# Moving two operands ahead of the last chunk's splits in the first quarter of an MLP, and two collections behind an operand in the last

## The chip, the cores and the metric

The kernel runs on one core of a Trainium2 chip. The metric is the device time of one execution in microseconds (us). The engines that matter are TensorE (PE, with its weight loads as PEld), VectorE (DVE), ScalarE (ACT), GpSimd (POOL) and SyncE (SP), each with its own queue of instructions that it takes in order; an instruction whose inputs or whose output buffer aren't ready holds up everything behind it on its engine.

## The reference

A two-layer encoder in float32 with S = 512 positions and a width of D = 1024. Layer 0 mixes with a stick-breaking attention, layer 1 with a gated linear recurrence (RG-LRU). The change touches the MLP that follows each of them:

```python
def squared_relu_mlp(h, w1, w2):
    u = jax.nn.relu(h @ w1)          # 512x1024 @ 1024x4096
    return (u * u) @ w2              # 512x4096 @ 4096x1024
...
        h = rms_norm(x, norm_mlp[layer])
        x = x + squared_relu_mlp(h, mlp_w1[layer], mlp_w2[layer])
    return rms_norm(x, norm_final)
```

## The kernel before

**Operands.** Every product is made from operands that are split in two halves: the high one is a cast on ACT (`wh`, `sh`, `bh`, `s`), the low one is what is left, a subtraction on DVE (`wl`, `sl`, `bl`, `low`). A product of a block takes three matmuls, high by high, low by high, high by low. So each operand costs one instruction on ACT and then one on DVE before PE can use it.

**Slots.** The halves of all weights live in tiles of the tags `wh` and `wl`. These come from one pool that has four slots for each tag (L91), and a new tile takes the slot of the tile four requests earlier, in the order in which the program requests them. The cast that fills a slot waits until PE has read the older tile for the last time.

**Quarters.** An MLP goes through the 4096 inner columns in four quarters (`q4` 0 to 3), the first of them in another form than the rest. In the first quarter `quarters` calls `squared` for eight chunks of 128 columns of `u`: 24 matmuls (`dense`, L236 to L238) with weights that `slab` loads, casts (L229, ACT) and subtracts (L231, DVE), then relu and square on ACT. After a pair of chunks `split` makes the halves of `u`, and `sums` forms differences of its parts for seven products (P1 to P7) that take the place of eight. `run` does what follows: the last chunk's `squared(C - 1)` with its splits and sums, the "down" products of the first quarter, and then "up" and "down" of the other three.

**Steps of `run`.** A down step multiplies one operand with the split `u` (12 matmuls of 128x512, recorded at L1107). `make(i)` builds the operand of step `i`: `operand` requests `wh` and `wl`, casts and subtracts. `add` forms a sum of two weight blocks `b` on DVE first, where the product needs one. `leave(i)` runs behind step `i`: it collects finished sums (`collect`: on DVE a multiply and add into `c` out of PSUM, or on ACT a scaled copy) and prepares the operand of step `i + 4`. Steps of the first quarter go P1 0, P5 0, P1 1, P2 0, P5 1 and so on (the number is the group of rows); steps of layer 1's last quarter go P1 0, P5 0, P1 1, P2 0, P5 1, P2 1, P6 0, P6 1, P3 0, P3 1, P7 0, P7 1, P4 0, P4 1.

**Order.** A scheduler places the instructions of each engine. Between `e.turn(True)` and `e.turn(False)` the MLP's own instructions on DVE and ACT are tied in the order in which the code issues them (`Ordered`); what is issued before that, and what doesn't go through `self.V` and `self.A` (the slab's L229 and L231 among it), may be placed between them. All operations that go through `Ordered` are recorded at L776, so they are told apart by their tiles.

In this text chunk 6 and chunk 7 are the last two chunks of `u` in the first quarter, and operands 0 to 4 are those of the first down steps.

Of the kernel before, what the change touches and what calls it, by code (L numbers as in the profile page):

```python
# [62 lines left out]
def hybrid_encoder(  # L63
# [72 lines left out]
    def x_down(*down):  # L136

        xgh.down = xgl.down = down
# [78 lines left out]
    behind = [None]  # L217
# [545 lines left out]
    NQ = DFF // D  # L763
# [22 lines left out]
    class Mlp:  # L786
# [357 lines left out]
        def run(self, first, between, end):  # L1144
# [13 lines left out]
            def place(i):  # L1158

                return (i + self.STEPS // 2) % self.STEPS  # L1160

            def unit(i):
                kind, q4, g, _ = steps[i]
                return units[kind, q4][g]
# [4 lines left out]
            def add(i, ahead=1):  # L1169

                if i >= len(steps) or i in done or steps[i][3] not in ("P5", "P6"):
                    return
                *what, name = steps[i]
                far = what[0] == "down" and (name, what[2]) in FARS
                if ahead > (5 if far else 2 if name == "P5" else what[0] == "up"):
                    return
                if steps.index((*what, {"P5": "P1", "P6": "P5"}[name])) in made:
                    done.add(i)

                    self.added(unit(i), name, far=far)  # L1180

            def make(i):
                if i >= len(steps):
                    return
                name = steps[i][3]
                ws[i] = made[i] = self.operand(self.source(unit(i), name))

                for before, x in (("P5", "P7"), ("P6", "P4")):
                    if name == before:
                        self.added(unit(i), x)  # L1190

            def prepare(i):

                if i < len(steps) and steps[i][0] == "up" and steps[i][3] == "P7":
                    return
                if i - 1 in range(len(steps)) and i - 1 not in made and i > 2:
                    make(i - 1)
                if i < len(steps) and steps[i][0] == "down":
                    add(i, 0)
                    if waiting and place(i) in (20, 22, 23):  # L1200
                        self.split_slot(*waiting.pop(0))
                make(i)
                for n in range(i + 1, i + 6):
                    add(n, n - i)

            def last_sums(u, which):
                for to, a, b, how in which:
                    self.V.tensor_tensor(u[to], u[a], u[b], how)
# [23 lines left out]
            def leave(i):  # L1232

                ahead = i + 4
                if i < 0:
                    return
                kind, q4, p, name = steps[i]
                bank = sums[kind, q4, p if kind == "up" else 0][self.PRODUCTS[name][3]]
                if kind == "down":
                    if q4 == 0 and self.s3 and place(i) in self.REPLACE:  # L1240
                        self.replace()
                    if p:
                        self.collect(name, 0, bank[0])
                    if steps[min(ahead, len(steps) - 1)][0] == "down":
                        add(ahead, 0)
                    if p:
                        self.collect(name, 1, bank[1])
                    prepare(ahead)
                    if later and place(i) > 15:
                        later.pop()()  # L1250
                    if q4 == 0:
                        x_down(FRONT, ASIDE)
                        if place(i) in self.LOWER:
                            self.lower(*self.LOWER[place(i)])

                        if self.layer == 0 and place(i) in (19, 20):
                            (self.sums_of_x, self.halves_of_sums)[place(i) - 19](3)
                    return
                u, three = us[p], bank.rearrange("p (i n) -> p i n", i=2)
                keep = {"P1": 0, "P6": 1, "P5": 2, "P7": 3}.get(name)  # L1260
                if keep is not None:

                    self.A.copy(u[keep], three)
                at, x, y, op = {
                    "P3": (1, three, u[1], ALU.subtract),
                    "P7": (2, u[2], u[3], ALU.subtract),
                    "P2": (0, u[0], three, ALU.add),
                    "P4": (3, three, None, None),
                }.get(name, (None,) * 4)
                if op:  # L1270
                    self.V.tensor_tensor(u[at], x, y, op)
                if name == "P4":
                    def fourth(u=u, three=three, p=p):
                        self.A.activation(u[3], three, AF.Relu)
                        self.square(u[3])
                        if p:
                            last_sums(u, self.SUMS[:2])
                        else:
                            self.sums(p, slice(0, 2))

                    if p:
                        fourth()
                    else:
                        later.append(fourth)
                elif later:
                    later.pop()()
                prepare(ahead)
                if op:
                    def rest(u=u, at=at):
                        self.A.activation(u[at], u[at], AF.Relu)  # L1290
                        self.square(u[at])
                        if p:
                            self.split_slot(p, u[at], at)

                    if p and name == "P3":
                        later.append(rest)
                    else:
                        rest()
                    if name == "P2" and not p:
                        self.split(p, slice(0, 2), slice(0, 3), slice(0, 3))  # L1300
                elif name == "P4" and p:
                    last_sums(u, self.SUMS[2:3])
                    self.split_slot(p, u[2], 5)
                    later.append(lambda: last_sums(u, self.SUMS[3:]))
                    waiting[:] = [(p, u[j], 3 + j) for j in (0, 1, 3)]
                elif name in ("P5", "P6") and p:
                    n = ("P5", "P6").index(name)
                    self.split(0, n, slice(0, 4), slice(3, 7))
# [3 lines left out]
            add(1)  # L1312
            make(1)
            add(5, 4)
            for e in (self.V, self.A):
                e.turn(True)
            self.squared(C - 1)
            self.split(1, 1, slice(0, 3), slice(0, 3))
            make(2)
            self.sums(1, 1)  # L1320
            make(3)
            add(4, 2)
            self.split(1, 1, slice(0, 4), slice(3, 7))
            between(C - 1)
            for i, (kind, q4, g, name) in enumerate(steps):
                load(i)
                leave(i - 1)
                if i == len(steps) - 2:
                    break
                if kind == "down":  # L1330
                    self.part(sums.setdefault((kind, q4, 0), {}), name, g, ws.pop(i))
                    continue
                if name == "P1":
                    us[g] = self.slots_of(g)
                banks = sums.setdefault((kind, q4, g), {})
                to = self.PRODUCTS[name][3]
                new = to not in banks
                if new:
                    banks[to] = self.bank()
                self.up(name, ws.pop(i), banks[to], new)  # L1340
# [490 lines left out]
```

## Time and profile before

| | before |
|---|---|
| time, median of 3 runs | 1032.02 us (1031.94 to 1032.03) |
| the profiled execution's own time | 1031.83 us |
| its span in the trace | 1030.1 us |
| mean granted TensorE clock | 0.999 |
| PE busy | 1021.6 us (99%) |
| PEld busy | 892.9 us (87%) |
| DVE busy | 859.7 us (83%) |
| ACT busy | 714.7 us (69%) |
| POOL busy | 173.9 us (17%) |

Rows of the timeline give the start in us from the span's start, the duration in us, engine, line, operation, the tile written and the tiles read, shapes and how many instructions the row groups; in brackets stands how long the engine was idle before it and what ended that. Rows of the chain of waits give start, duration, engine, tile and line. PE's matmuls overlap in the records: their starts, not their durations, tell the rate.

### The profile page before, as it was taken

Reading aid. Unit: us, or ns where it says so; the run is one execution under the profiler, and the core shown is the slowest. Engines: PE = TensorE matmul, PEld = TensorE weight load, DVE = VectorE, ACT = ScalarE, POOL = GpSimd, SP = SyncE. Lnnn points to the kernel's source line nnn. Section 1 sums busy time; section 2 is a strip of 40 time slices with the busy share of each in tenths; the row PEclk is TensorE's granted clock in tenths of the full one; section 3 lists DMA queues with packets and bytes.
Section 4 is the critical chain, followed back from the end, with each engine's and each line's share of the span. In section 5 each row is a group of like instructions: output and inputs, shape, how many; then the busy total and the mean of one; then the engine's idle time right before and its main releaser. Section 6 shows DMA issues by size and latency. Waiting matters only on the chain.

```text
span 1030.1 us, 15892 instructions
## 1 busy us (share of the span) xinstructions
PE 1021.6 (99%) x5868; PEld 892.9 (87%) x5868; DVE 859.7 (83%) x1152; ACT 714.7 (69%) x1108; POOL 173.9 (17%) x235
## 2 busy tenths in 40 slices
PE   9999999999999999999999999999999999999997
PEld 7888888888888988988988888888878988988986
DVE  7878787847889799798899889984788798798898
ACT  6777676835877774774875689964866774874866
POOL 0444344420010010010011110300000010010012
PEclk9999999999999999999999999999999999999999
DMA  7745454537536677677682564452437677667653
GB/s 239 216 120 144 106 154 104 153 111 262 156 82 195 164 164 190 162 163 193 164 227 80 150 171 128 103 204 87 98 80 190 163 161 192 169 154 197 163 126 105
DMA packets 52700, 159.41 MB, mean 155 GB/s; under 512 B 6672, under 2 KB 7952, under 8 KB 52624
## 3 DMA queue, kind: packets, MB, share of 16 engines
q1 hardware_dynamic: 41376, 119.35, 36.0%
q0 software_dynamic: 10528, 38.28, 22.0%
q8 instruction: 46, 0.75, 0.3%
q10 hardware_dynamic: 720, 0.79, 0.2%
q14 instruction: 30, 0.25, 0.1%
HBM read 137.41 MB, written 4.19 MB: 137 GB/s over the span
## 4 chain that ended last, share of the span: by engine, by line
PE 92%; DVE 3%; ACT 2%; DMA 1%; issue 1%; POOL 0%; SPq 0%; DVEq 0%; ACTq 0%
PE ps_t L1107 15%; PE ps_acc L1012 10%; PE ps_z L1012 8%; PE ps_acc L1107 7%; PE ps_acc L236 5%; PE ps_acc L238 5%; PE ps_acc L237 5%; PE ps_o L1012 5%; PE ps_z L1107 4%; PE ps_t L236 3%; PE ps_t L237 3%; PE ps_t L238 3%; PE ps_o L236 2%; PE ps_o L237 2%; PE ps_o L238 2%; PE ps_t L622 1%
## 5 line engine op out<-in xcount | busy, mean ns | idle before, releaser
L776 ACT CAST wh<-b 128x1024 fp32r<-128x1024 f32 x168 | 174.2, 1051 | 108.0 <-DVE b L776 65.6
L776 DVE TENSOR_TENSOR wl<-b,wh 128x1024 fp32r<-128x1024 f32 x168 | 204.1, 1220 | 45.7 <-ACT wh L776 45.1
L1089 POOL DMA_DIRECT2D b<-in_w_dn x40 | 35.0, 876 | 352.2 <-DVE b L776 155.1
L236 PE MATMUL ps_acc<-xg,wh 128*128 128x512 f32 x208 | 84.8, 408 | 0.0
L238 PE MATMUL ps_acc<-xg,wh 128*128 128x512 f32 x208 | 81.4, 392 | 0.0
L237 PE MATMUL ps_acc<-xg,wl 128*128 128x512 f32 x208 | 81.4, 391 | 0.0
L1012 PE MATMUL ps_z<-xg,wh 128*128 128x256 f32 x384 | 78.8, 277 | 0.0
L231 DVE TENSOR_TENSOR wl<-raw,wh 128x512 fp32r<-128x512 f32 (+2 forms) x70 | 61.6, 905 | 15.7 <-ACT wh L229 15.7
L600 DVE TENSOR_TENSOR_SCAN scan<-keep,later 128x128 f32<-128x128 f32 (+1 forms) x64 | 58.9, 922 | 16.9 <-ACT keep L590 11.5
L776 ACT ACTIVATE u<-u 128x512 f32<-128x512 f32 x100 | 63.1, 632 | 9.1 <-DVE u L776 7.5
L229 ACT CAST wh<-raw 128x512 fp32r<-128x512 f32 (+2 forms) x70 | 50.7, 759 | 24.5 <-PE ps_acc L238 7.3
L1012 PE MATMUL ps_z<-xg,wl 128*128 128x256 f32 x240 | 66.3, 276 | 0.0
L1012 PEld LDWEIGHTS ps_z<-xg,wh 128*128 128x128 f32 x384 | 62.7, 188 | 0.1
L1012 PE MATMUL ps_acc<-xg,wh 128*128 128x256 f32 x288 | 61.4, 277 | 0.0
L604 POOL TENSOR_TENSOR w<-w,scan 128x128 f32<-128x128 f32 (+1 forms) x64 | 51.8, 811 | 56.4 <-DVE scan L600 53.5
L1089 POOL DMA_DIRECT2D b<-in_w_up x24 | 20.9, 870 | 237.7 <-DVE b L776 108.1
L776 DVE TENSOR_TENSOR b<-b,b 128x1024 f32<-128x1024 f32 x48 | 58.7, 1223 | 1.3
L776 DVE TENSOR_TENSOR u<-u 128x512 f32<-128x512 f32 (+1 forms) x92 | 54.8, 596 | 2.4 <-ACT u L776 1.1
L1012 PE MATMUL ps_acc<-xg,wl 128*128 128x256 f32 x192 | 53.1, 277 | 0.0
L1012 PE MATMUL ps_acc<-low,wh 128*128 128x256 f32 x192 | 53.0, 276 | 0.0
L776 ACT CAST wh<-raw 128x1024 fp32r<-128x1024 f32 x46 | 47.9, 1044 | 7.3 <-PE ps_acc L1107 7.3
L1107 PE MATMUL ps_t<-wh,bh 128*128 128x512 f32 x126 | 49.2, 391 | 0.2 <-DVE c L776 0.2
(383 smaller groups left out, 3268.7 us busy)
## 6 DMA issues: line engine op xcount, KB each, us to landing
b<-in_w_dn SPq DMA_DIRECT2D x48, 512.0 KB, 4.6
b<-in_w_dn POOLq DMA_DIRECT2D x40, 512.0 KB, 5.5
b<-in_w_up SPq DMA_DIRECT2D x36, 512.0 KB, 4.6
b<-in_w_up POOLq DMA_DIRECT2D x24, 512.0 KB, 5.5
raw<-in_w_m SPq DMA_DIRECT2D x16, 512.0 KB, 4.6
raw<-in_w_dn SPq DMA_DIRECT2D x16, 512.0 KB, 4.6
raw<-in_w_in SPq DMA_DIRECT2D x16, 512.0 KB, 4.6
raw<-in_w_qk SPq DMA_DIRECT2D x12, 512.0 KB, 3.9
```

Of the source, the lines that this page charges most:

```text
L229: A.copy(wh[:, k, :], raw[:, k, :])
L231: V.tensor_tensor(wl[:, k, :], raw[:, k, :], f(wh[:, k, :]), ALU.subtract)
L236: PE.matmul(ps, wh, ah, start=start, stop=False)
L237: PE.matmul(ps, wl, ah, start=False, stop=False)
L238: PE.matmul(ps, wh, al, start=False, stop=stop)
L600: V.tensor_tensor_scan(sc[:, S - n : S][:, ::-1], keep[:, :n][:, ::-1], later[:, S - n :][:, ::-1], 1.0, ALU.mult, ALU.max,)
L604: G.tensor_tensor(wt, wt, sc[:, S - n + 1 : S + 1], ALU.mult)
L622: PE.transpose(tr[:, (qb - kb) * P : (qb - kb + 1) * P], w[pair, j, qb][:, kb * P : (kb + 1) * P], ident,)
L776: ins = getattr(self.e, name)(*args, **kwargs)
L1012: PE.matmul(ps[:, i * HS : (i + 1) * HS], m, y, start=new and i == k == n == 0, stop=i == 1 and k == C // 2 - 1 and n == 2, skip_group_che ...
L1089: G.dma_start(out=unit[b].rearrange("p j n -> p (j n)"), in_=unit["src"](to), accum_op=ALU.add)
L1107: PE.matmul(ps, m, y[:, jj, cols], start=first and n == 0, stop=last and n == 2, skip_group_check=not new,)
```

## The change

Two edits, with lines numbered as in the kernel before.

The first is in `run`, for both layers. `make(2)` moves from behind the last chunk's first split to the place ahead of `e.turn(True)`, and so ahead of `squared(C - 1)`; `make(3)` moves from behind `sums(1, 1)` to the place between `squared(C - 1)` and the first split. The second is in `leave`, for layer 1's last quarter alone: behind step P2 1 both collections are issued after the next operand has been prepared, where before one stood ahead of `add` and one between `add` and `prepare`.

```diff
@@ leave @@
-                    if p:
+                    behind = p and name == "P2" and self.layer and q4 == NQ - 1
+                    if p and not behind:
                         self.collect(name, 0, bank[0])
                     if steps[min(ahead, len(steps) - 1)][0] == "down":
                         add(ahead, 0)
-                    if p:
+                    if p and not behind:
                         self.collect(name, 1, bank[1])
                     prepare(ahead)
+                    if behind:
+                        for n in range(2):
+                            self.collect(name, n, bank[n])
@@ run @@
             add(1)
             make(1)
             add(5, 4)
+            make(2)
             for e in (self.V, self.A):
                 e.turn(True)
             self.squared(C - 1)
+            make(3)
             self.split(1, 1, slice(0, 3), slice(0, 3))
-            make(2)
             self.sums(1, 1)
-            make(3)
             add(4, 2)
```

PE's and SP's instructions keep their order. On ACT two places of layer 1's first quarter move. The first is behind chunk 5's relu (`u<-ps_o`); `wh_7782<-raw` is the weights of chunk 7, `wh_7779<-b11` is operand 2.

```order
 L776 CAST s3_7598<-x_5858 128x256
 L776 ACTIVATE u_7423<-ps_o_7669 128x512
-L229 CAST wh_7782<-raw_7780 128x1024
+L776 CAST wh_7779<-b11_7430 128x1024
 L776 CAST bh_78<-x_5858 128x256
 L776 CAST s3_7660<-x_5860 128x256
```

Operand 2 stands where chunk 7's weights stood. The second place is behind chunk 6's relu (`u<-ps_t`); `raw_7784` with `wh_7786` is chunk 7's weights under their new numbers.

```order
 L776 CAST sh_7702<-u_7423 128x768
 L776 ACTIVATE u_7423<-ps_t_7726 128x2x256
+L229 CAST wh_7786<-raw_7784 128x1024
 L776 CAST s3_7660<-x_5862 128x256
 L776 ACTIVATE u_7423<-u_7423 128x2x256
```

The cast of chunk 7's weights now stands behind the relu of chunk 6. On DVE, at the same place, `wl_7787<-raw_7784` is the low half of chunk 7's weights.

```order
 L776 TENSOR_TENSOR sl_7703<-u_7423,sh_7702 128x768
 L776 TENSOR_TENSOR x_5862<-x_5870,x_5862 128x256
+L191 TENSOR_SCALAR rr_7764<-rr_7764 128x4
+L231 TENSOR_TENSOR wl_7787<-raw_7784,wh_7786 128x1024
 L776 TENSOR_TENSOR low_7718<-x_5862,s3_7660 128x256
-L191 TENSOR_SCALAR rr_7764<-rr_7764 128x4
 L776 TENSOR_TENSOR u_7423<-u_7423 128x256
```

The low half of chunk 7's weights comes behind a subtraction for chunk 6's `u` and one for `x`. Layer 0 moves in the same way. In layer 1's last quarter, on DVE, `wl_10225<-b22` (before: `wl_10227`) is the operand of P3 1, and `c0<-ps_z` are the two collections of P2 1.

```order
 L776 TENSOR_TENSOR sl_10020<-u_9851,sh_10019 128x2x256
 L776 TENSOR_TENSOR wl_10207<-b22_9981,wh_10206 128x1024
+L776 TENSOR_TENSOR sl_10020<-u_9853,sh_10019 128x2x256
+L776 TENSOR_TENSOR wl_10225<-b22_9983,wh_10224 128x1024
 L776 SCALAR_TENSOR_TENSOR c0_7352<-ps_z_10170,rr_7764,c0_7352 128x512
 L776 SCALAR_TENSOR_TENSOR c0_7352<-ps_z_10171,rr_7764,c0_7352 128x512
-L776 TENSOR_TENSOR sl_10020<-u_9853,sh_10019 128x2x256
-L776 TENSOR_TENSOR wl_10227<-b22_9983,wh_10226 128x1024
```

The operand of P3 1 passes ahead of both collections.

## Prediction

> **What bounds the kernel now.** I read the page first, then the timeline of PE for starts that lie further apart than the rest, then ACT and DVE at those places. The page's chain that ended last says what sets the time:
>
> ```profile
> PE 92%; DVE 3%; ACT 2%; DMA 1%; issue 1%; POOL 0%; SPq 0%; DVEq 0%; ACTq 0%
> ```
>
> PE carries the chain, and what DVE and ACT have of it are the places at which PE runs dry. So an edit counts by what it does to PE's idle time, and by nothing else. How fast PE goes when it is fed shows in a down step of the chain:
>
> ```profile
> 769.26 5.44 PE ps_t L1107 x24
> ```
>
> 24 matmuls of 128x512 take 5.44 us, 0.227 us each. A start later than that behind the one before is a stall. The first edit works on stalls of this kind in the first quarter; two places in layer 1 and two in layer 0; the second edit works on one in the last quarter:
>
> ```profile
> 759.80 0.39 PE L1107 MATMUL ps_t<-wh,sh 128*128 128x512 f32 x1
> 760.08 0.50 PE L1107 MATMUL ps_t<-wl,sh 128*128 128x512 f32 x1
> ...
> 765.54 0.39 PE L1107 MATMUL ps_acc<-wh,sh 128*128 128x512 f32 x1
> 766.47 0.50 PE L1107 MATMUL ps_acc<-wl,sh 128*128 128x512 f32 x1 [0.54 <-DVE wl L776]
> 766.81 0.39 PE L1107 MATMUL ps_acc<-wh,sl 128*128 128x512 f32 x1
> ...
> 302.18 0.39 PE L1107 MATMUL ps_acc<-wh,sh 128*128 128x512 f32 x1
> 302.60 0.50 PE L1107 MATMUL ps_acc<-wl,sh 128*128 128x512 f32 x1
> ...
> 324.04 0.39 PE L1107 MATMUL ps_z<-wh,sl 128*128 128x512 f32 x1
> 324.66 0.47 PE L1107 MATMUL ps_t<-wh,bh 128*128 128x512 f32 x1 [0.23 <-DVE c L776]
> ...
> 1009.45 0.39 PE L1107 MATMUL ps_acc<-wh,sh 128*128 128x512 f32 x1
> 1009.88 0.50 PE L1107 MATMUL ps_acc<-wl,sh 128*128 128x512 f32 x1
> ```
>
> Each time the second matmul of a step waits for the low half `wl`, and the third follows the second by 0.34 instead of 0.227 (766.47 to 766.81): a stall costs about 0.11 more than its wait.
>
> **First edit, what it gives.** In layer 1 the largest stall is 766.47: 0.93 + 0.34 − 2 × 0.227 = 0.81 us, at operand 4. DVE there is a queue without a hole:
>
> ```profile
> 756.79 2.10 DVE L776 TENSOR_TENSOR sl<-u,sh 128x1024 fp32r<-128x1024 f32 x2 [2.08 <-ACT sh L776]
> 758.81 1.22 DVE L776 TENSOR_TENSOR wl<-b,wh 128x1024 fp32r<-128x1024 f32 x1
> ...
> 761.66 1.22 DVE L776 TENSOR_TENSOR wl<-raw,wh 128x1024 fp32r<-128x1024 f32 x1
> ...
> 765.19 2.36 DVE L776 TENSOR_TENSOR wl<-b,wh 128x1024 fp32r<-128x1024 f32 x2
> ```
>
> Two of these subtractions, operand 2 (758.81) and operand 3 (761.66), now come earlier: operand 2's ahead of chunk 7 altogether, which frees 1.22 us of this queue, and operand 3's ahead of most of it. Operand 4 (the first of the two at 765.19) ends 1.2 us earlier or more against its PE, where 0.93 − 0.23 = 0.70 is late. So 766.47 goes, and 760.08 (0.28 + 0.34 − 0.45 = 0.17) with it, because operand 2 is long done: −0.98 us, and I add −0.2 for smaller stalls between them and up to the next quarter, an estimate with bounds 0 and −0.4. In layer 0 the stall at 302.60 goes in the same way, 0.42 + 0.34 − 0.45 = −0.31, and that at 324.66 (0.62 − 0.23 = 0.39) shrinks, since ACT and DVE are ahead by an operand: −0.3, bounds 0 and −0.39. What is late next is operand 3 for its own step: its subtraction now sits between the two of the row at 756.79, so against PE it ends where 756.79 + 1.05 + 1.22 = 759.1 was, and its step began one step of 2.72 behind 759.80, at 762.5. That is no stall.
>
> **First edit, what it takes.** The move of `make(2)` ahead of `squared(C - 1)` also moves the request for its slot. Requests used to be: chunk 5, chunk 6, operand 0, operand 1, chunk 7, operand 2. With four slots chunk 7 took the slot of chunk 5. Now operand 2 takes that of chunk 5, and chunk 7's weights get the slot of chunk 6, which PE reads up to the last matmul before chunk 7 begins. That chunk's weights can't be cast until PE has nothing else left. Before, in layer 1:
>
> ```profile
> 743.96 1.05 ACT L229 CAST wh<-raw 128x1024 fp32r<-128x1024 f32 x1
> 749.34 0.61 ACT L776 ACTIVATE u<-ps_t 128x512 f32<-128x512 f32 x1
> 749.83 0.42 ACT L776 CAST s<-x 128x256 fp32r<-128x256 f32 x1
> ...
> 745.93 1.22 DVE L231 TENSOR_TENSOR wl<-raw,wh 128x1024 fp32r<-128x1024 f32 x1
> 751.14 0.42 DVE L776 TENSOR_TENSOR x<-x 128x256 f32<-128x256 f32 x1
> 751.48 0.42 DVE L776 TENSOR_TENSOR low<-x,s 128x256 fp32r<-128x256 f32 x1
> ...
> 748.78 0.49 PE L236 MATMUL ps_acc<-xg,wh 128*128 128x512 f32 x1
> 749.10 0.40 PE L237 MATMUL ps_acc<-xg,wl 128*128 128x512 f32 x1
> ```
>
> The cast ended at 745.0 and the subtraction at 747.2, ahead of the first use at 748.78. By the new order the cast stands behind chunk 6's relu (749.34), so it starts where the next ACT instruction did, at 749.83, and ends at 750.88. The subtraction stands behind `x<-x` (751.14) and a short L191, so it starts at about 751.55 and ends at 752.77. PE's second matmul moves from 749.10 to 752.8, and the third follows by 0.34 instead of 0.24: +3.8 us. Bounds: if DVE takes it as soon as the cast is done, 750.9 + 1.2 = 752.15, so +3.15; if one more subtraction of 0.42 comes ahead of it, +4.2. Everything behind chunk 7 shifts with PE.
>
> In layer 0 the same happens with shorter queues:
>
> ```profile
> 285.10 0.60 ACT L776 ACTIVATE u<-ps_z 128x512 f32<-128x512 f32 x1 [0.17 <-PE ps_z L238]
> 285.60 0.40 ACT L776 CAST bl<-x 128x256 fp32r<-128x256 f32 x1
> ...
> 287.09 0.42 DVE L776 TENSOR_TENSOR u<-u 128x256 f32<-128x256 f32 x1
> ...
> 285.71 0.49 PE L236 MATMUL ps_o<-xg,wh 128*128 128x512 f32 x1
> 286.04 0.40 PE L237 MATMUL ps_o<-xg,wl 128*128 128x512 f32 x1
> ```
>
> The cast starts at 285.60 and ends at 286.65; the subtraction takes the place behind the next `u`, at 287.1, and ends at 288.3. PE's second matmul moves from 286.04 to 288.34, and 0.1 comes on top: +2.4 us, bounds +1.9 (DVE right behind the cast, 286.65 + 1.22 = 287.87) and +2.8.
>
> SP issues its transfers in the same order. The raw tiles of the two operands and of chunk 7 rotate as before, so no load comes later for PE; POOL has nothing there.
>
> **Second edit.** In the last quarter DVE and ACT do this ahead of the stall at 1009.88:
>
> ```profile
> 1006.69 1.40 DVE L776 SCALAR_TENSOR_TENSOR c<-ps_z,rr,c 128x512 f32<-128x512 f32 x2
> 1008.61 2.36 DVE L776 TENSOR_TENSOR wl<-b,wh 128x1024 fp32r<-128x1024 f32 x2
> ...
> 1006.79 1.05 ACT L776 CAST wh<-b 128x1024 fp32r<-128x1024 f32 x1 [0.45 <-PE ps_t L1107]
> 1009.65 1.05 ACT L776 CAST wh<-b 128x1024 fp32r<-128x1024 f32 x1 [0.86 <-PE ps_acc L1107]
> ```
>
> With the two collections (1.40) behind it, the operand's subtraction waits only for its cast (1007.84) and ends at 1009.06 instead of 1009.83. PE gets there at 1009.45 + 0.23 = 1009.68, so the stall goes: 0.43 + 0.34 − 0.45 = −0.31 us. What is late next is the second subtraction of that row: it ends at 1009.06 + 1.32 + 1.2 = 1011.6, and its step begins at 1012.2. On ACT the reading of `c` moves to 1010.4 and is done before the cast that waits for PE at 1012.72 by the same count of steps. So nothing else moves. If that cover were gone, at most 0.3 comes back.
>
> **The sum.** +2.4 − 0.31 − 0.3 + 3.8 − 0.98 − 0.2 − 0.31 = +4.1. On the profiled execution's own 1031.83 us that makes 1035.9; the median before lies 0.19 above that execution, so I say 1036.0. With the low bounds of both new stalls and the largest savings it is 1032.02 + 1.9 + 3.15 − 0.31 − 0.39 − 0.98 − 0.4 − 0.31 = 1034.7; with the high ones and the smallest savings, 1032.02 + 2.8 + 4.2 − 0.31 − 0.98 − 0.31 = 1037.4.
>
> **Rivals.** *The savings don't come.* After the new stalls ACT and DVE could be as late against PE as before, because the work of the last chunk is pushed back by as much as PE: 1032.02 + 6.2 = 1038.2. Against it speaks that two operands are out of the queue and that nothing was put in.
>
> *The clock falls.* In layer 1 PE would do a single matmul between 748.8 and 752.8. The end of the kernel shows what idleness does:
>
> ```profile
> 1023.46 0.28 PE L1107 MATMUL ps_o<-wh,sl 128*128 128x256 f32 x1
> ...
> 1023.50:1027.50 4.00, 0.23 (x2) 0.03 (x1) 2.73 (x7) 2.40 (x6) 0.00 (x0) 1.00 0.46 172
> 1027.50:1030.00 2.50, 0.00 (x0) 0.00 (x0) 0.00 (x0) 0.00 (x0) 0.00 (x0) 0.54 0.41 152
> ```
>
> The granted clock (third from the end) was still 1.00 over the 4 us behind the last matmul, and 0.54 after them. Were a stall of 4 us enough, and did the clock stay near half for another 4 us, PE would lose about 2 us: 1038.0. One matmul in the middle speaks against it, and so does 1.00 over a stretch as long as this one. [...]
>
> *Faster.* If chunk 7's weights are cast in time, only the savings are left: 1032.02 − 0.31 − 0.3 − 0.98 − 0.2 − 0.31 = 1029.9. It decides whether the cast is done before PE gets to 748.78 (285.71 in layer 0); for that the slot would have to be free by 747.7, while chunk 6's own matmuls run. The order on ACT, with the cast behind chunk 6's relu, speaks against it.
>
> **How the numbers follow.** The forecast, both new stalls and the savings: 0.75. No savings: 0.08. The clock falls: 0.12. The weights in time: 0.05, of which 0.03 faster and 0.02 with some of the savings lost, within 0.2%. About 0.2%, or 2.06 us, is what a measurement of this kernel can tell from no change. Faster 0.03, same 0.04 (0.02 more from the forecast's own lower edge), slower 0.93. The range, 1034.5 to 1038.3, holds the forecast between its bounds and the two slower rivals.
>
> **What would show it.** In the trace after, L229 of chunk 7 behind the relu of chunk 6 in both layers, then a gap of PE of 3.7 us more at L236 and L237 in layer 1, and 2.3 in layer 0; no start further than 0.3 apart in the first three down steps behind, nor where 766.47, 302.60 and 1009.88 stood; the clock at 1.00 behind 753. I am wrong if L229 comes before the relu, if the stalls of the down steps move instead of going, or if the clock drops.

## The result: 1039.35 us, slower by 0.7%

| | before | after |
|---|---|---|
| median of 6 runs | 1031.74 us | 1039.35 us |
| lowest to highest | 1030.99 to 1032.03 | 1037.24 to 1039.94 |
| the profiled execution | 1031.83 us | 1039.65 us |
| its span | 1030.1 us | 1037.9 us |
| mean granted TensorE clock | 0.999 | 0.995 |

The ratio is 1.0072, with a 95% interval of 1.0059 to 1.0085. The kernel went the way that was forecast, by 7.6 us instead of 4.1, and out of the range. Two things in the table ask for a reason: the lower clock, and a spread of 2.7 us where the kernel before has 1.0.

The profile after, first PE in its timeline in layer 0, at the place where 285.71 and 286.04 stood before. In brackets is the wait.

```profile
284.49 0.94 PE L183 MATMUL ps_z<-ones,ssq 128*128 128x1 f32 x8
286.27 0.50 PE L236 MATMUL ps_o<-xg,wh 128*128 128x512 f32 x1 [0.83 <-ACT wh L229]
287.96 0.50 PE L237 MATMUL ps_o<-xg,wl 128*128 128x512 f32 x1 [1.19 <-DVE wl L231]
288.30 0.39 PE L238 MATMUL ps_o<-xg,wh 128*128 128x512 f32 x1
...
289.21 0.60 PE L236 MATMUL ps_o<-xg,wh 128*128 128x512 f32 x1
289.62 0.63 PE L237 MATMUL ps_o<-xg,wl 128*128 128x512 f32 x1
...
292.18 0.61 PE L237 MATMUL ps_o<-xg,wl 128*128 128x512 f32 x1
292.60 0.42 PE L238 MATMUL ps_o<-xg,wh 128*128 128x512 f32 x1
```

The first three rows are the stall that was forecast: the high half and then the low half of chunk 7's weights come late. The rows behind it were not forecast. From 289.62 to 292.18 matmuls start 0.427 apart (2.56 / 6) instead of 0.227, with no wait in brackets. The same in layer 1, PE first and then the ACT and DVE rows that it waited for:

```profile
754.28 0.79 PE L236 MATMUL ps_acc<-xg,wh 128*128 128x512 f32 x1 [2.01 <-ACT wh L229]
756.16 0.79 PE L237 MATMUL ps_acc<-xg,wl 128*128 128x512 f32 x1 [1.10 <-DVE wl L231]
756.76 0.63 PE L238 MATMUL ps_acc<-xg,wh 128*128 128x512 f32 x1
...
760.17 0.44 PE L237 MATMUL ps_acc<-xg,wl 128*128 128x512 f32 x1
760.45 0.40 PE L238 MATMUL ps_acc<-xg,wh 128*128 128x512 f32 x1
...
752.69 0.60 ACT L776 ACTIVATE u<-ps_t 128x512 f32<-128x512 f32 x1
753.18 1.04 ACT L229 CAST wh<-raw 128x1024 fp32r<-128x1024 f32 x1
...
754.49 0.42 DVE L776 TENSOR_TENSOR x<-x 128x256 f32<-128x256 f32 x1
754.90 1.22 DVE L231 TENSOR_TENSOR wl<-raw,wh 128x1024 fp32r<-128x1024 f32 x1
```

The cast stands behind chunk 6's relu and the subtraction behind `x<-x`, as worked out. Busy time by stretches of the same kernel, with the granted clock third from the end:

```profile
748.00:752.00 4.00, 4.00 (x23) 3.42 (x22) 3.90 (x8) 4.00 (x10) 0.00 (x0) 1.00 0.13 28
752.00:756.00 4.00, 1.06 (x4) 0.46 (x3) 4.00 (x10) 3.36 (x7) 0.00 (x0) 0.68 0.01 2
756.00:760.00 4.00, 3.83 (x9) 3.06 (x10) 3.15 (x9) 1.41 (x2) 0.00 (x0) 0.50 0.49 131
760.00:764.00 4.00, 4.00 (x18) 3.23 (x18) 1.23 (x1) 0.63 (x2) 0.00 (x0) 0.97 0.00 0
```

PE is busy 1.06 of 4.00 us in the stall, the clock falls inside it, and stays at 0.50 over the next 4 us, in which PE does 9 matmuls where the stretch ahead of the stall had 23.

**The difference added up.** What the lower clock costs is read from the starts. In layer 0, from 289.21 to 292.60, eight steps take 3.39 us instead of 8 × 0.227 = 1.82, so 1.57 are lost. In layer 1, from 756.16 to 760.45, ten steps take 4.29 us instead of 0.34 + 9 × 0.227 = 2.38, so 1.91 are lost. That is 3.48 us. The profiled executions differ by 7.82; without the clock's part 4.34 are left, beside the forecast's +4.1.

### The profile page after: what moved, and what is told of

Its sections match the earlier page's. It is cut to its first block, busy times and chain, and to the rows that moved or that the text cites. A ratio compares the mean times of both kernels' runs of the same rounds, so it can differ in the third digit from the quotient of the medians.

```text
span 1037.9 us, 15889 instructions
## 1 busy us (share of the span) xinstructions
PE 1024.8 (99%) x5868; PEld 895.6 (86%) x5868; DVE 860.7 (83%) x1152; ACT 714.6 (69%) x1108; POOL 169.5 (16%) x235
## 4 chain that ended last, share of the span: by engine, by line
PE 93%; DVE 3%; ACT 2%; DMA 1%; issue 1%; POOL 0%; SPq 0%; DVEq 0%; ACTq 0%
PE ps_t L1107 16%; PE ps_acc L1012 9%; PE ps_acc L1107 8%; PE ps_z L1012 8%; PE ps_acc L237 5%; PE ps_acc L238 5%; PE ps_acc L236 5%; PE ps_o L1012 5%; PE ps_z L1107 4%; PE ps_t L236 2%; PE ps_t L237 2%; PE ps_t L238 2%; PE ps_o L237 2%; PE ps_o L236 2%; PE ps_o L238 2%; PE ps_t L622 1%
## 5 line engine op out<-in xcount | busy, mean ns | idle before, releaser
L237 PE MATMUL ps_acc<-xg,wl 128*128 128x512 f32 x208 | 82.3, 395 | 1.1 <-DVE wl L231 1.1
L776 DVE TENSOR_TENSOR wl<-raw,wh 128x1024 fp32r<-128x1024 f32 x38 | 46.2, 1218 | 9.6 <-ACT wh L776 9.5
```

The lines of the kernel that those rows point to most:

```text
L237: PE.matmul(ps, wl, ah, start=False, stop=False)
L776: ins = getattr(self.e, name)(*args, **kwargs)
```

## Experiments

Each time that is compared is against runs of the kernel before on the same chip. Two theories: the stalls come from the slot that chunk 7's weights get (and not from operand 2's work ahead of chunk 7), and the rest of the loss is the clock's answer to the stalls. The rival to the first is that operand 2 itself holds up ACT and DVE; the rival to the second that the stalls cost 7 us by themselves.

### The slot or the work

`slab_first`, the changed kernel with two requests exchanged:

```diff
+            self.last = slab(w_m1[self.layer, C - 1])   # and dense() takes these halves for chunk 7
             make(2)
             for e in (self.V, self.A):
                 e.turn(True)
```

> The changed kernel, but chunk 7's weights are requested just ahead of operand 2, so that they get chunk 5's slot again and operand 2 gets chunk 6's. If the slot is the cause: no gap of PE at L236 and L237 of chunk 7, clock 0.999, and only the savings are left, 1031.7 - 1.9 = 1029.8 us (1029.3 to 1031.0). If the work of operand 2 itself ahead of chunk 7 is the cause: the gaps stay, 1036 us or more.

1030.98 us, ratio 0.9992 (0.9984 to 1.0001). PE at chunk 7 of layer 1 and the casts on ACT, from its timeline:

```profile
748.54 0.49 PE L236 MATMUL ps_acc<-xg,wh 128*128 128x512 f32 x1
748.86 0.40 PE L237 MATMUL ps_acc<-xg,wl 128*128 128x512 f32 x1
...
743.72 1.04 ACT L229 CAST wh<-raw 128x1024 fp32r<-128x1024 f32 x1
749.10 0.59 ACT L776 ACTIVATE u<-ps_t 128x512 f32<-128x512 f32 x1
749.59 1.04 ACT L776 CAST wh<-b 128x1024 fp32r<-128x1024 f32 x1
```

Chunk 7's cast is back at 743.72 and operand 2's stands behind chunk 6's relu, where it harms nobody: no stall, no lower clock. Operand 2 is still made ahead of chunk 7's relu and splits on both engines. So the order of the two requests makes the loss. That it does so by way of the slot rests on the places of the tiles in the built programs (below); a kernel with a fifth slot was not run. The gain is less than expected, since the stall at operand 4 is down to 0.47 in layer 1 and still there, and the one in layer 0 (302.60 before) is 0.58.

`make2_only`, the kernel before with the one line moved:

```diff
             add(5, 4)
+            make(2)
             for e in (self.V, self.A):
                 e.turn(True)
             self.squared(C - 1)
             self.split(1, 1, slice(0, 3), slice(0, 3))
-            make(2)
             self.sums(1, 1)
```

> The kernel before, with make(2) alone moved ahead of the last chunk. If the request order of that one operand makes the stalls: both gaps and the lower clock are there as in the changed kernel, 1039 to 1040.5 us. If make(3) or the collections have part in them: under 1037 us.

1040.02 us, ratio 1.0067 (1.0051 to 1.0082), with both stalls. One line carries the loss.

### The clock

`filler`, the changed kernel with matmuls that PE does while it would wait:

```diff
+                ps = self.bank()
+                if c == C - 1:
+                    for n in range((5, 10)[self.layer]):
+                        PE.matmul(ps, xgh[:, 0, :P], xgh[:, 0, :], start=True, stop=True)
+                ps = dense(w_m1[self.layer, c], xgh, xgl, ps=ps)
```

> The changed kernel, with 5 (layer 0) and 10 (layer 1) additional matmuls of 128x512 just ahead of chunk 7, into its PSUM bank, which its first real matmul starts anew; PE does them while it would wait. If the stalls cost about 6.2 us, the savings give back 1.9 and the rest of the loss is the clock's: the clock stays at 1.00 and the time is 1031.7 + 4.2 = 1036 us (1035.3 to 1036.7), with less spread between runs than the changed kernel's 2.7 us. If the stalls themselves are worth the whole loss: 1039.3 us.

1036.66 us (1036.38 to 1037.16), ratio 1.0044 (1.0031 to 1.0056). Its timeline in layer 0, and its stretches in layer 1:

```profile
285.40 0.95 PE L183 MATMUL ps_z<-ones,ssq 128*128 128x1 f32 x8
286.21 1.42 PE L863 MATMUL ps_o<-xg 128*128 128x512 f32 x5
287.46 0.40 PE L236 MATMUL ps_o<-xg,wh 128*128 128x512 f32 x1
288.87 0.50 PE L237 MATMUL ps_o<-xg,wl 128*128 128x512 f32 x1 [1.01 <-DVE wl L231]
...
752.00:756.00 4.00, 2.75 (x13) 1.94 (x12) 4.00 (x10) 2.30 (x5) 0.00 (x0) 1.00 0.01 2
756.00:760.00 4.00, 4.00 (x19) 3.29 (x18) 2.85 (x7) 1.67 (x2) 0.00 (x0) 1.00 0.44 131
```

The wait for chunk 7 is as long as without them (L183 to L237 3.47 us, as 284.49 to 287.96 above, and in layer 1 4.86 beside 4.84), but the clock stays at 1.00. The ratio is 1.0044 instead of 1.0072, some 2.9 us less, and the two intervals don't overlap; the spread is 0.8 us. This shows the clock's part as a part of its own. What is left, 4.5 us above the kernel before on the same chip, is near the 4.1 that were forecast for the stalls and the savings together.

`fill_one`, with these matmuls in layer 1 alone, was to tell whether layer 0's shorter stall lowers the clock by itself:

```diff
-                    for n in range((5, 10)[self.layer]):
+                    for n in range((0, 10)[self.layer]):
```

> The changed kernel with additional matmuls of 128x512 (10) ahead of chunk 7 in layer 1 alone; layer 0's stall stays empty. If the clock answers to each stall by itself: no row under 1.00 behind layer 1's stall, and some under 1.00 behind layer 0's, where PE idles about 2.8 us with one matmul in between; the time is between the two, 1036.7 + 1.6 = 1038.3 us (1037.5 to 1039). If a stall under 3 us doesn't lower it: 1036.7.

1036.11 us (1035.21 to 1037.61), ratio 1.0039 (1.0024 to 1.0055). The profiled execution had no lower clock, against the expectation, though the stall was the same. So I ran it again, the changed kernel twice more, and one with the filling in layer 0 alone (`range((5, 0)[self.layer])`).

> The changed kernel once more, for the place of the lower clock. If the clock is set for stretches of 3.41 us by how busy PE was in the stretch before, on a grid that lies anew in each execution: behind layer 1's stall of 4 us one or two stretches at 0.5 (some 1.7 us each), behind layer 0's of 2.8 us none, one or two, by where the grid lies. If every stall of over 1.5 us lowers it in the same way: the same rows at 0.5 as in the first trace, 3.4 and 6.8 us.

> As the run before it: the lengths at 0.5 differ between executions if the grid's place decides, and don't if the stall alone does.

> The changed kernel with additional matmuls ahead of chunk 7 in layer 1 alone, once more. If the grid decides: some executions have one or two stretches at 0.5 behind layer 0's stall (time near 1037.5 or 1039), some none (near 1035.7). If a stall of 2.8 us with a matmul in it doesn't lower the clock: near 1035.7 again.

> The changed kernel with additional matmuls ahead of chunk 7 in layer 0 alone (5); layer 1's stall of 4 us with one matmul in it stays empty. In every place of a 3.41 us grid some stretch is less than half busy: one or two stretches at 0.5 behind it, 1038 to 1040 us, and none in layer 0.

The same stall of layer 0 in two executions of one program, `fill_one` and then `fill_one_a`, busy time in two stretches from 285 on:

```profile
285.00:288.40 3.40, 1.38 (x6) 0.90 (x7) 3.40 (x9) 2.44 (x5) 0.00 (x0) 1.00 0.00 0
288.40:291.80 3.40, 3.40 (x16) 2.78 (x15) 2.25 (x6) 1.05 (x1) 0.00 (x0) 1.00 0.54 158
```

```profile
285.00:288.40 3.40, 1.38 (x7) 0.89 (x7) 3.40 (x9) 2.49 (x5) 0.00 (x0) 0.94 0.00 0
288.40:291.80 3.40, 3.40 (x10) 2.68 (x9) 2.25 (x6) 1.05 (x1) 0.00 (x0) 0.55 0.52 157
```

PE is busy 1.38 of 3.40 us in both; the clock of the second falls to 0.55 in the next stretch, and PE does 10 matmuls there instead of 16. The trace's clock records give how long it lasts; the loss is worked out from the starts as above:

| profiled execution | time | at 0.5 behind layer 0's stall | behind layer 1's | lost by the starts | time without it |
|---|---|---|---|---|---|
| the changed kernel | 1039.65 | 3.41 us | 6.83 us | 3.48 | 1036.2 |
| `after_a` | 1038.77 | none | 6.83 us | 2.85 | 1035.9 |
| `after_b` | 1038.92 | none | 6.83 us | 2.78 | 1036.1 |
| `fill_one` | 1035.74 | none | filled, none | 0 | 1035.7 |
| `fill_one_a` | 1037.54 | 3.41 us | filled, none | 1.56 | 1036.0 |
| `fill_other` | 1039.62 | filled, none | 6.83 us | 2.74 | 1036.9 |
| `make2_only` | 1041.73 | 6.83 us | 6.83 us | 4.90 | 1036.8 |

In these executions the lower clock lasted 3.41 or 6.83 us; behind layer 0's stall it came for 6.83 us, for 3.41 or not at all, behind layer 1's for 6.83 us each time that stall was left empty. The lengths change between executions of one program, and the time without the lost part hardly does (the executions come from several chips, on which the kernel before took 1031.7 to 1032.2 us). In the trace of the changed kernel the clock changes at 289.23, 292.64, 753.44, 760.27 and 1036.75 us from the span's start, in each case whole multiples of 3.413 us from the others (289.23 to 753.44 is 136 of them).

So PE's rows can be counted in the 3.41 us ahead of each change, and in the others on the same steps. 15 matmuls of 128x512 fit there at 0.227 apart, and 8 at 0.427. For `fill_one_a` the place comes from the mean clock of its stretches, to 0.1 us.

| trace | stretch, us from the span's start | matmuls of 128x512 begun in it | clock in the 3.41 us behind it |
|---|---|---|---|
| `fill_one_a`, layer 0 | 284.6 to 288.0 | 2 | 0.50 |
| the changed kernel, layer 0 | 285.82 to 289.23 | 7 | 0.50 |
| | 289.23 to 292.64 | 8 | 1.00 |
| the changed kernel, layer 1 | 750.03 to 753.44 | 5 | 0.50 |
| | 753.44 to 756.86 | 3 | 0.50 |
| | 756.86 to 760.27 | 8 | 1.00 |

The clock fell with single waits of 0.83 and 1.19 us in layer 0, behind a stretch in which seven matmuls had begun. These rows give no rule. In `fill_one` two matmuls began between 284.6 and 288.0 as well, at 286.15 and 287.84, and the clock stayed at 1.00. At the end of the changed kernel eleven matmuls of 128x256 from 1029.92 to 1033.33 were followed by 1.00. PE's busy time doesn't sort them either: 2.23 of 3.41 us ahead of 753.44 were followed by 0.50, 1.55 from 1029.92 on by 1.00. That such steps lie elsewhere against the stall in `fill_one` than in `fill_one_a`, and that this makes the difference, is the author's estimate from the equal stalls and the unequal clocks; it was not shown. What exactly is counted was not tried.

### The second edit

`collect_only`, the kernel before with the edit in `leave` alone.

> The kernel before, with the second edit alone. By the prediction: the stall at 1009.88 goes and nothing else moves, -0.3 us, 1031.4 us. By the rival, that the collections come late somewhere behind (the changed kernel's trace has a new gap of 0.38 at 1025.61): 1031.6 to 1031.7 us.

1031.85 us, ratio 0.9998 (0.9989 to 1.0007). This interval holds no change and the forecast −0.3 us alike, so the trace has to tell. Its timeline, DVE and then PE:

```profile
1006.79 1.22 DVE L776 TENSOR_TENSOR wl<-b,wh 128x1024 fp32r<-128x1024 f32 x1
1007.93 1.40 DVE L776 SCALAR_TENSOR_TENSOR c<-ps_z,rr,c 128x512 f32<-128x512 f32 x2
1009.25 1.21 DVE L776 TENSOR_TENSOR wl<-b,wh 128x1024 fp32r<-128x1024 f32 x1
...
1016.42 0.74 DVE L776 SCALAR_TENSOR_TENSOR c<-ps_t,rr,c 128x512 f32<-128x512 f32 x1
...
1016.88 0.39 PE L1107 MATMUL ps_t<-wh,sl 128*128 128x512 f32 x1
1017.31 0.47 PE L1107 MATMUL ps_t<-wh,bh 128*128 128x512 f32 x1
1017.62 0.39 PE L1107 MATMUL ps_t<-wl,bh 128*128 128x512 f32 x1
```

The same place before, the collection and then PE's start in the next bank:

```profile
1016.92 0.74 DVE L776 SCALAR_TENSOR_TENSOR c<-ps_t,rr,c 128x512 f32<-128x512 f32 x1
...
1017.96 0.40 PE L1107 MATMUL ps_t<-wh,bh 128*128 128x512 f32 x1
```

The stall of P3 1 is gone, and a new one of 0.43 + 0.31 − 0.45 = 0.29 us stands at 1017.31: PE starts in a bank of `ps_t` 0.15 us behind the end of a collection out of `ps_t` (1016.42 + 0.74 = 1017.16). DVE has no idle time between the two places, so its collection ends no earlier, whatever the order; PE got there 0.3 us sooner and waits as much. That the bank is what it waits for is read from the times, not tried.

### Where a gain is

`both_behind` keeps the request order of before and makes both operands directly behind the last chunk:

```diff
             self.squared(C - 1)
+            make(2)
+            make(3)
             self.split(1, 1, slice(0, 3), slice(0, 3))
-            make(2)
             self.sums(1, 1)
-            make(3)
```

> The kernel before, with make(2) and make(3) both directly behind squared(C - 1), so that the request order is the one of before. If only the slot makes the new stalls: no gap at chunk 7 and the clock stays. But both operands then stand ahead of chunk 7's splits on ACT and DVE, which the third step needs: a new gap of up to 2 us there by the durations of before (two casts of 1.05), less in part for operand 4. 1031.5 to 1033.5 us.

1031.81 us, ratio 0.9999 (0.9990 to 1.0008). No stall at chunk 7; the third step waits for its `sl` (0.50 between starts), and operand 4 comes as late as before (0.93 between starts). So this new order within the same full queue gains nothing.

`early2` is the kernel before with chunk 7's weights requested first and operand 2 ahead of chunk 7, and nothing else moved.

> The kernel before, with chunk 7's weights requested first and then operand 2 made ahead of chunk 7; make(3) and the collections as before. If operand 2's way out of the full queue behind chunk 7 is what saves: about the time with both moved, ratio 0.999 to 0.9995. If make(3)'s place mattered: no gain, 1.000.

1031.05 us, ratio 0.9989 (0.9980 to 0.9998): operand 2's way out of the queue brings a small gain, and operand 3's place nothing that could be told from `slab_first`. Layer 1's stall at operand 4 is at 0.50 between starts, layer 0's unchanged at 0.42.

`early3` takes one more piece of DVE work from behind chunk 7, the sum of weights for operand 4:

```diff
+            self.last = slab(w_m1[self.layer, C - 1])
+            make(2)
+            add(4, 2)
             for e in (self.V, self.A):
                 e.turn(True)
             self.squared(C - 1)
             self.split(1, 1, slice(0, 3), slice(0, 3))
-            make(2)
             self.sums(1, 1)
             make(3)
-            add(4, 2)
```

> As the kernel before with chunk 7's weights requested first and operand 2 made ahead of chunk 7, and the sum of weights for operand 4 (add(4, 2), 1.22 us of DVE) ahead of chunk 7 too. If DVE's queue behind chunk 7 is what bounds operand 4: the stalls at operand 4 go in both layers, 0.81 and 0.31 us, and the ratio is 0.998 to 0.999. If ACT's chain bounds it, or chunk 7's splits are pushed back: 0.9992 or more.

1030.01 us, ratio 0.9977 (0.9968 to 0.9987), the one version that clearly beats the kernel before. DVE and PE in layer 1, at what was 766.47:

```profile
752.91 1.22 DVE L776 TENSOR_TENSOR b<-b,b 128x1024 f32<-128x1024 f32 x1
...
761.12 1.22 DVE L776 TENSOR_TENSOR sl<-u,sh 128x1024 fp32r<-128x1024 f32 x1
762.26 2.35 DVE L776 TENSOR_TENSOR wl<-b,wh 128x1024 fp32r<-128x1024 f32 x2
...
764.12 0.39 PE L1107 MATMUL ps_acc<-wh,sh 128*128 128x512 f32 x1
764.35 0.39 PE L1107 MATMUL ps_acc<-wl,sh 128*128 128x512 f32 x1
764.58 0.39 PE L1107 MATMUL ps_acc<-wh,sl 128*128 128x512 f32 x1
```

The sum is made at 752.91, while PE works on chunk 7; operand 4's `wl` ends at 762.26 + 1.2 = 763.5, ahead of its use at 764.35, and the three starts are 0.23 apart. The stall of layer 0 at operand 4 is gone too.

## Why the prediction was wrong, step by step

- **The new stall in layer 1**, +3.8: right. The starts at 731.87 before and 735.21 after (one chunk that the edit doesn't touch) were 3.34 apart, those of chunk 7's second matmul 756.16 − 749.10 = 7.06, so +3.72, and 0.1 on top.
- **The new stall in layer 0**, +2.4: right. L183 to L237 is 287.96 − 284.49 = 3.47 instead of 1.14, so +2.33, and 0.1 on top (before, L183 stood at 284.90). What was wrong is one sentence of the kernel's description: a tile doesn't take the slot of the tile four requests earlier, but that of the tile given back first. Operand 3 had chunk 7's slot before. For chunk 7 both give the same, and in the built programs its `wh` lies where chunk 5's lay before, and where chunk 6's lies after.
- **The savings in the first quarter**, −0.31, −0.3, −0.98 and −0.2: about right. In the trace after, no gap is left at operand 4 in either layer, and that at 324.66 is down from 0.62 to 0.29 between starts. They came with PE held back by the new stalls; without these (`slab_first`) operand 4 is late again in both layers. So the reason given, two operands out of DVE's queue, does not suffice by itself, and that the size fits all the same is in part luck. Without the new stalls the gap at operand 4 went only when the sum for it left the queue as well (`early3`). That the stalls gave DVE and ACT the time that was lacking is likely, and not tried by itself. The gap at 324.66 was also counted among the waits for a low half; by its row it is the first matmul of a step, behind a collection (`<-DVE c`).
- **The second edit**, −0.31: wrong, by the traces next to nothing (0.31 saved, 0.29 lost again in `collect_only`). The step "what is late next" looked at the next subtraction alone. DVE was full up to 1017.66, and the next that PE took from it beyond its operands, a bank after a collection, had only 0.3 us to spare.
- **"The clock falls"**, 0.12 and +2: this is what happened, beside the stalls, and in both layers. The step that failed is the argument against it, by which the sum put this term at nothing and counted PE's idle time alone: a matmul in the middle, and 1.00 over the 4 us behind the kernel's last matmul. In that trace 0.50 begins at 1027.68, 4.22 us behind the start of the last matmul at 1023.46. In the changed kernel's layer 0 it begins at 289.23, with 1.6 us of waits in the 3.41 us ahead of it (0.45 up to 286.27, and 1.19). The 3.48 us are lost while PE works, with starts 0.427 apart. And the fall was priced once, at 2.0, where up to 6.83 us at 0.5 came in each layer: 2.8 to 4.9 us were lost in all, in the traces with both stalls open. With it at 3.48 the forecast of 1036.0 becomes 1039.5.

## What to carry to other kernels

Moving an instruction also moves its request for a buffer: before an operand goes ahead, write down which tiles are requested in which order, and whose slot each gets then. The stalls here, 2.0 us of waits in layer 0 and 3.1 in layer 1, cost more than their length where the clock fell for the 3.4 or 6.8 us behind them (1.57 and 1.91 us more in the changed kernel's trace). So price such a stall by both, and give the range the executions in which the clock doesn't fall. Where DVE's queue was full, a new order in it only moved a wait; what shortened it was work that left that stretch of the queue.

## What the runs showed of the hardware

In the changed kernel's trace the granted clock went between 1.0 and 0.5 at times that lie whole multiples of 3.413 us apart, and it was at 0.5 for 3.41 us behind layer 0's stall and 6.83 us behind layer 1's. In the 3.41 us ahead of 0.5 PE had begun seven, five and three matmuls of 128x512, and eight in each of the two ahead of the return to 1.0. In layer 0, waits of 0.83 and 1.18 to 1.19 us with one matmul between them were followed by 0.5 in `fill_one_a` and not in `fill_one`, one program. In layer 1, where the changed kernel's waits were 2.01 and 1.10 us, 0.5 followed in all five traces in which the stall was left empty. With ten matmuls without use in the first part of the wait the clock stayed at 1.00 in all three traces that have them in layer 1, where the empty wait cost 1.9 to 2.9 us more than its length.
